# Attention scores computed two at a time, and attention's pieces placed inside the weight products

## The chip, the cores and the metric

The kernel runs on one NeuronCore of one Trainium2 chip. TensorE (PE in the profile; PEld is its weight load) multiplies, VectorE (DVE) and ScalarE (ACT) work element by element and read the products out of PSUM, GpSimd (POOL) does small sums, and the DMA queues bring the weights in. The metric is device time in microseconds (us), the median over runs of the whole program.

## The reference, cut to what matters

Two layers of a first block, then one second block, on a sequence of 256 tokens, 1024 wide, in fp32. A layer of the first block has a differential attention with 8 heads (two components of 64 each), a recurrent unit, a memory attention and an MLP. The second block has four attentions with 4 heads of 64 each.

```python
def diff_attention(q, k, v, lam, subln_g, lam_init):     # first block: 8 heads, two layers
    mask = key_chunk[None, :] <= q_chunk[:, None]         # chunks of 64 tokens, blocks of 128 queries
    s1 = jnp.einsum('bhqd,bhkd->bhqk', qb[0], k1).astype(jnp.float32) * scale
    s2 = jnp.einsum('bhqd,bhkd->bhqk', qb[1], k2).astype(jnp.float32) * scale
    p1 = jax.nn.softmax(jnp.where(mask, s1, NEG_BIG), axis=-1)
    p2 = jax.nn.softmax(jnp.where(mask, s2, NEG_BIG), axis=-1)
    p = p1 - lam * p2                                     # then p @ v

# second block: four branches of 4 heads each
o_sb = stick_breaking_attention(q, k, v)                  # strict causal, products of 1 - sigmoid
o_mb = moba_attention(q, k, v, t5_bias[:, :4])            # at this length one causal block with a bias
o_fx = forgetting_attention(q, k, v, f_logit)             # causal, plus sums of log f
o_ds = dsa_attention(q, k, v, q_idx, k_idx, w_idx, t5_bias[:, 4:])   # best 64 keys of an indexer, one k for all heads
```

## The kernel before

The weights are 267 blocks of up to 128 x 2048, in a fixed order (`plan`). For each block ScalarE rounds the block to fp32r (`wh`) and VectorE takes what is left over (`wl`); a product of a block is three passes on TensorE, `hi,wh`, `lo,wh` and `hi,wl`, which are 48 instructions of 128x256 for most blocks (24 of 128x512 for those that give token-major results). `step` emits one block: it reads out the last block's product (`flush`), lets light jobs run (`run_light`), lets up to `SEGS` = 3 attention pieces run (`run_heavy`), splits weights up to two blocks ahead (`pump`), and then emits the block's product (`mm`). The instructions of an engine are issued in the order in which they are emitted here.

An attention job is a Python generator: each `yield` ends a piece. For the differential attention (`attn_pair`, two heads) the pieces are scores of head 0; scores of head 1 and probabilities of head 0; transposes; the product with V; and so on. `run_heavy` walks through the waiting jobs in order of priority and runs one piece of each that has waited for `GAP` = 2 steps, unless the estimated lag of VectorE behind TensorE is over `ROOM`. So all pieces of a step stand in a row ahead of the step's product. `need` runs pieces of one branch without products between them until the branch is done.

Scores: queries and keys lie feature-major, so a head's (or a component's) 64 features are 64 of the 128 partitions. For each head or component there are two products, block t=0 (128 keys) and t=1 (256 keys), which use 64 rows of the PE array. The two components of a differential head, and the two heads of a pair in the second block, lie in the lower and the upper 64 partitions of the same tiles (`qk`; in the second block `f`). In block 1 the mask is a product with one row: `uvb[0:1]` holds a 1 for the first 64 queries and NEG for 64 keys, and it is added after each of the two products. In the second block masks are products of the identity `identb` with a bf16 mask (`diag`: `strictb`, `causalb`; or `add`, the choice of the indexer).

An fp32 product shows as two instructions in the trace, one of fp32r or bf16 as one. All calls go through one recording helper, so every instruction has that helper's line (L289 before) and groups are told apart by tiles. `ps` is a PSUM bank, from a pool of 8.

Of the kernel before, what the change touches and what calls it, by code (L numbers as in the profile page):

```python
# [19 lines left out]
NEG = -1e30  # L20
# [5 lines left out]
# ---------------------------------------------------------------- host side layout  # L26
# [43 lines left out]
def constants():  # L70
# [12 lines left out]
    u = np.zeros((128, 128), np.float32)  # L83
    u[0, :64] = 1.0
    v = np.zeros((128, 64), np.float32)
    v[0, :] = NEG
# [8 lines left out]
    c["cst"] = np.concatenate([ident, ident[::-1], rope, causal, strict, u, v], axis=1)  # L95
# [157 lines left out]
class Meter:  # L253
    """Passes an engine's calls on and books them on the clock."""
# [52 lines left out]
class Prog:  # L307
# [7 lines left out]
    def __init__(self, tc, A, out, pools):  # L315
# [10 lines left out]
        self.run_no = 0  # L326
        self.turned = []
        self.G = []

    # ---- tiles  # L330
# [12 lines left out]
    # ---- weight stream  # L343
# [37 lines left out]
    # ---- pacing  # L381
# [13 lines left out]
    def run_heavy(self, force=None):  # L395
        n = 0
        for h in list(self.heavy):
            if force is not None:
                if h[4] not in force:
                    continue  # L400
            elif n == self.SEGS or self.late() > self.ROOM:
                break
            elif self.clock - h[1] < h[3]:
                continue
            n += 1
            h[1] = self.clock
            if next(h[2], "end") == "end":
                self.heavy.remove(h)

# [5 lines left out]
    def step(self, mm, ev=None, early=None):  # L415
# [4 lines left out]
        self.run_heavy()  # L420
        self.clock += 1
        self.pump()
        mm()
# [35 lines left out]
    # ---- arithmetic helpers  # L459
# [17 lines left out]
    def mm_w2(self, banks, w, X, nk=8, p0=0, first=True, last=True, outer=False):  # L477
        """As mm_w, with a bank for each of the two blocks of columns; outer: one block after the other."""
# [81 lines left out]
    # ---- start  # L560
    def setup(self):
# [7 lines left out]
        cst = cp.tile([128, 960], F, name="cst")  # L569
# [34 lines left out]
        self.uvb = cp.tile([128, 192], BF, name="uvb")  # L604
# [6 lines left out]
    def setup_lam(self):  # L611
# [4 lines left out]
        nc.vector.tensor_copy(self.uvb, cst[:, 768:960])  # L616
# [46 lines left out]
    # ---- memory keys and values  # L663
# [36 lines left out]
    # ---- block 1  # L700
# [25 lines left out]
    def attn_pair(self, l, p, Q, K, V, Y):  # L726
# [208 lines left out]
    def wmany(self, key, js, X, ev, order, early=None):  # L935
        """Chunks js at once; order: (chunk, pair of rows) as they are multiplied."""
# [330 lines left out]
    # ---- block 2  # L1267
# [98 lines left out]
    def sb_head(self, h, Q, K, V, st):  # L1366
# [387 lines left out]
```

## Time and profile before

| | |
|---|---|
| runs, us | 1678.87 median of 3 (1678.62 to 1685.62) |
| the profiled execution | span 1679.4 us, 0.5 us above the median of the runs |
| PE busy | 1648.2 us (98%), 12400 instructions |
| DVE, ACT, POOL busy | 1057.0 (63%), 879.8 (52%), 98.0 (6%) |
| mean granted TensorE clock | 0.981 of full |
| DMA | 277.51 MB, 165 GB/s on the mean |

How to read it: PE is busy from end to end, so time is in what PE does and how densely it can do it; an average over the span says little of any one stage, and the stretches with attention have to be read by themselves. Matmuls overlap, so sums of their durations exceed the span; the distance from one start to the next is what a matmul costs.

### The profile page before, as it was taken

To read this page: it belongs to the slowest core of one execution; us is meant where nothing else is said; L and a number is where in the kernel's file an instruction comes from. 1 tells how busy PE (TensorE), PEld (TensorE's weight loads), DVE (VectorE), ACT (ScalarE), POOL (GpSimd) and SP (SyncE) were. 2 spreads that over 40 slices of the span, in tenths; PEclk is the share of its full clock that TensorE was granted. 3 is DMA by queue.
4 is the path that set the end of the run, shared out by engine and by line. 5 is a ranking of instruction groups with operands and counts; after the bars stand their busy time and mean duration, and the time that the engine had idled before them with its cause. 6 is when DMAs were issued, how large, how long until landed. Compare 5 with 4: busy or idle time off the path is not lost.

```text
span 1679.4 us, 28920 instructions
## 1 busy us (share of the span) xinstructions
PE 1648.2 (98%) x12400; PEld 1562.5 (93%) x12400; DVE 1057.0 (63%) x1400; ACT 879.8 (52%) x1207; POOL 98.0 (6%) x84
## 2 busy tenths in 40 slices
PE   8999999999999999999999999999999999999998
PEld 7887999999999998888999999999889998999997
DVE  6675676756755346756767656554377756578863
ACT  6344495545566345454864446653345544356542
POOL 1100000001100002000001102000120000000000
PEclk9998899999999999988999999999999999999999
DMA  8643244455445555432354543555434432436551
GB/s 299 217 161 124 76 151 151 160 193 207 170 177 188 188 203 215 160 126 76 126 170 166 202 176 144 183 201 176 164 127 174 164 138 101 175 133 220 179 179 70
DMA packets 42408, 277.51 MB, mean 165 GB/s; under 512 B 4800, under 2 KB 4936, under 8 KB 10536
## 3 DMA queue, kind: packets, MB, share of 16 engines
q1 hardware_dynamic: 41768, 274.21, 46.2%
q8 instruction: 97, 1.59, 0.4%
q0 software_dynamic: 512, 1.46, 0.3%
q14 instruction: 31, 0.25, 0.0%
HBM read 274.59 MB, written 1.06 MB: 164 GB/s over the span
## 4 chain that ended last, share of the span: by engine, by line
PE 90%; DVE 3%; issue 3%; ACT 2%; POOL 2%; DMA 0%; POOLq 0%; DVEq 0%; SPq 0%; ACTq 0%
PE ps L289 90%; POOL sq L289 1%; ACT wh L289 1%; DVE wl L289 1%; DVE x L289 0%; DVE lo L289 0%; ACT hi L289 0%; ACT sq L289 0%; DMA mem<-in_memT_dram 0%; DVE h L289 0%; ACT rl L289 0%; DVE at L289 0%; DVE g L289 0%; DVE isc L289 0%; DVE yg L289 0%
## 5 line engine op out<-in xcount | busy, mean ns | idle before, releaser
L289 PE MATMUL ps<-hi,wh 128*128 128x256 f32 x3312 | 949.6, 287 | 2.0 <-ACT hi L289 2.0
L289 PE MATMUL ps<-hi,wl 128*128 128x256 f32 x3312 | 941.0, 284 | 2.6 <-DVE wl L289 2.6
L289 PE MATMUL ps<-lo,wh 128*128 128x256 f32 x3312 | 938.4, 283 | 2.3 <-DVE lo L289 2.3
L289 DVE TENSOR_TENSOR wl<-ws,wh 128x2048 fp32r<-128x2048 f32 (+2 forms) x267 | 587.4, 2206 | 384.5 <-ACT wh L289 383.9
L289 PEld LDWEIGHTS ps<-hi,wh 128*128 128x128 f32 x3312 | 631.4, 191 | 6.1 <-ACT hi L289 2.6
L289 PEld LDWEIGHTS ps<-lo,wh 128*128 128x128 f32 x3312 | 632.0, 191 | 3.4 <-DVE lo L289 3.1
L289 PEld LDWEIGHTS ps<-hi,wl 128*128 128x128 f32 x3312 | 629.7, 190 | 3.4 <-DVE wl L289 3.4
L289 ACT ACTIVATE wh<-ws 128x2048 fp32r<-128x2048 f32 (+2 forms) x267 | 484.7, 1822 | 235.5 <-PE ps L289 212.1
L289 PE MATMUL ps<-wh,hi 128*128 128x512 f32 (+1 forms) x288 | 116.0, 403 | 8.9 <-ACT wh L289 7.0
L289 POOL TENSOR_TENSOR sq<-sq 128x512 f32<-128x512 f32 (+1 forms) x42 | 70.8, 1685 | 777.9 <-ACT sq L289 776.0
L289 PE MATMUL ps<-wh,lo 128*128 128x512 f32 (+1 forms) x288 | 114.4, 397 | 0.0
L289 PE MATMUL ps<-wl,hi 128*128 128x512 f32 (+1 forms) x288 | 114.3, 397 | 0.0
L289 PEld LDWEIGHTS ps<-wh,hi 128*128 128x128 f32 x288 | 55.8, 194 | 20.7 <-ACT wh L289 7.0
L289 PEld LDWEIGHTS ps<-wh,lo 128*128 128x128 f32 x288 | 55.5, 193 | 12.6 <-DVE lo L289 0.2
L289 PEld LDWEIGHTS ps<-wl,hi 128*128 128x128 f32 x288 | 55.8, 194 | 11.9 <-DVE wl L289 0.4
L289 DVE TENSOR_TENSOR lo<-rl,hi 128x512 fp32r<-128x512 f32 x32 | 23.3, 727 | 52.5 <-ACT hi L289 52.5
L289 DVE TENSOR_REDUCE at<-ps 128x1 f32<-128x128 f32 (+2 forms) x80 | 27.9, 386 | 44.6 <-PE ps L289 44.6
L289 ACT ACTIVATE rl<-ps 128x512 f32<-128x512 f32 (+1 forms) x40 | 22.6, 574 | 62.4 <-PE ps L289 62.4
L289 PE MATMUL ps<-ah,wh 128*128 128x256 f32 x176 | 49.7, 282 | 0.0
L289 PE MATMUL ps<-al,wh 128*128 128x256 f32 x176 | 49.6, 282 | 0.0
L289 PE MATMUL ps<-ah,wl 128*128 128x256 f32 x176 | 49.6, 282 | 0.0
L289 ACT ACTIVATE gz<-ps,hb 128x256 f32<-128x256 f32 x48 | 20.1, 469 | 49.5 <-PE ps L289 42.5
(230 smaller groups left out, 1337.1 us busy)
## 6 DMA issues: line engine op xcount, KB each, us to landing
ws<-in_up_dram SPq DMA_DIRECT2D x54, 1024.0 KB, 4.8
ws<-in_inw_dram SPq DMA_DIRECT2D x48, 1024.0 KB, 4.8
ws<-in_dn_dram SPq DMA_DIRECT2D x32, 1024.0 KB, 4.8
ws<-in_inq_dram SPq DMA_DIRECT2D x24, 1024.0 KB, 4.8
ws<-in_g_dram SPq DMA_DIRECT2D x16, 1024.0 KB, 4.9
ws<-in_wo_dram SPq DMA_DIRECT2D x12, 1024.0 KB, 4.8
ws<-in_in2f_dram SPq DMA_DIRECT2D x9, 1024.0 KB, 4.9
ws<-in_kvk_dram SPq DMA_DIRECT2D x8, 1024.0 KB, 5.4
```

The source lines that it names most:

```text
L289: return fn(*a, **k)
```

## The change

It does three things.

1. Scores in pairs. The products of two components (block 1) or two heads (second block) are emitted alternately into two banks: t=0 of the lower rows, t=0 of the upper rows, t=1 of the lower, t=1 of the upper. The second block's jobs are now for two heads each (`sb_heads`, `fox_heads`, `t5_heads`), with half as many jobs and pieces of twice the size.
2. Full-row masks. Block 1's mask is now `identb` times `lateb` (128 rows, 64 columns), and the four masks of a head follow after all its products, where each used to follow its product.
3. Pieces inside products. `run_heavy` runs one piece per call. It is called once ahead of the product, as before, and again inside it, when a third and two thirds of it have been passed.

```diff
     def run_heavy(self, force=None):
-        n = 0
+
         for h in list(self.heavy):
             if force is not None:
                 if h[4] not in force:
                     continue
-            elif n == self.SEGS or self.late() > self.ROOM:
+            elif self.late() > self.ROOM:
                 break
             elif self.clock - h[1] < h[3]:
                 continue
-            n += 1
             h[1] = self.clock
             if next(h[2], "end") == "end":
                 self.heavy.remove(h)
+            if force is None:
+                break
...
         self.run_heavy()
+        self.pump()
+        self.parts = [(n + 1) / self.SEGS for n in range(self.SEGS - 1)]
+        mm()
+        self.parts = []
         self.clock += 1
-        self.pump()
-        mm()
...
     def mid(self, part):
+        if self.parts and part >= self.parts[0] and part < 1.0:
+            self.parts.pop(0)
+            self.run_heavy()
...
         def scores(h):
             c0 = 4 * h
+            ss = [self.ps(), self.ps()]
+            for t in range(2):
+                o, n = 128 * t, 128 * (t + 1)
+                for c in range(2):
+                    rows = slice(c * 64, (c + 1) * 64)
+                    nc.tensor.matmul(ss[c][:, o:o + n], lhsT=q[rows, h, t * 128:(t + 1) * 128], rhs=k[rows, h, :n],
+                                     start=t == 0, stop=False, skip_group_check=True)
             for c in range(2):
-                s = self.ps()
-                rows = slice(c * 64, (c + 1) * 64)
                 for t in range(2):
-                    o, n = 128 * t, 128 * (t + 1)
-                    nc.tensor.matmul(s[:, o:o + n], lhsT=q[rows, h, t * 128:(t + 1) * 128], rhs=k[rows, h, :n],
-                                     start=t == 0, stop=False, skip_group_check=True)
-                    nc.tensor.matmul(s[:, o + n - 64:o + n], lhsT=self.uvb[0:1, 0:128], rhs=self.uvb[0:1, 128:192],
-                                     start=False, stop=True, skip_group_check=True)
+                    o = 256 * t + 64
+                    nc.tensor.matmul(ss[c][:, o:o + 64], lhsT=self.identb, rhs=self.lateb, start=False, stop=True,
+                                     skip_group_check=True)
+            for c in range(2):
+                s = ss[c]
...
-    def qk_scores(self, s, q, k, h, kk=None):
-        i, rows = divmod(h, 2)
-        rows = slice(rows * 64, rows * 64 + 64)
+    def qk_scores(self, q, k, i, kk=None):
+
+        ss = [self.ps(), self.ps()]
         for t, o, n in self.SEG:
-            self.nc.tensor.matmul(s[:, o:o + n], lhsT=q[rows, i, t * 128:(t + 1) * 128],
-                                  rhs=k[rows, i if kk is None else kk, :n],
-                                  start=t == 0, stop=False, skip_group_check=True)
+            for r in range(2):
+                rows = slice(r * 64, r * 64 + 64)
+                self.nc.tensor.matmul(ss[r][:, o:o + n], lhsT=q[rows, i, t * 128:(t + 1) * 128],
+                                      rhs=k[rows, i if kk is None else kk, :n],
+                                      start=t == 0, stop=False, skip_group_check=True)
+        return ss
...
+    def head_tail(self, i, ee, V, st, scale=1.0):
+        PT = [self.p_transpose(e, scale) for e in ee]
+        yield
+        for r in range(2):
+            self.attn_out(st, 2 * i + r, PT[r], V(2 * i + r))
...
-        for h in range(4):
-            self.spawn(self.t5_head(h, FT["dsq"], FT["kk"], lambda h: [VB[t][:, 256:320] for t in range(2)], 4, box,
+        for i in range(2):
+            self.spawn(self.t5_heads(i, FT["dsq"], FT["kk"], lambda h: [VB[t][:, 256:320] for t in range(2)], 4, box,
                                     BR[3]), 4, tag=3)
```

PE's rows in the first block, where the first scores of layer 0 stand. Before, behind the transposes of rotated keys (`rz`), two heads follow each other ahead of the next product; this is the first of them (`ps` numbers are banks by name, `LDWEIGHTS` loads a bf16 operand).

```order
L289 MATMUL ps_1236<-cst_86,rz_1093 128x128 x4
L289 MATMUL ps_1247<-qk_776,qk_727 128x128
L289 LDWEIGHTS uvb_109
L289 MATMUL ps_1247<-uvb_109 128x64
L289 MATMUL ps_1247<-qk_776,qk_727 128x256
L289 LDWEIGHTS uvb_109
L289 MATMUL ps_1247<-uvb_109 128x64
L289 MATMUL ps_1258<-qk_776,qk_727 128x128
L289 LDWEIGHTS uvb_109
L289 MATMUL ps_1258<-uvb_109 128x64
L289 MATMUL ps_1258<-qk_776,qk_727 128x256
```

The same head now stands inside the product into `ps_1167` (`hi` and `lo` are the activations, `wh` and `wl` the weights), with 18 more instructions of that product behind it, and then the other head.

```order
L287 MATMUL ps_1167<-hi_908,wl_1082 128x256
L287 MATMUL ps_1200<-qk_776,qk_727 128x128
L287 MATMUL ps_1201<-qk_776,qk_727 128x128
L287 MATMUL ps_1200<-qk_776,qk_727 128x256
L287 MATMUL ps_1201<-qk_776,qk_727 128x256
L287 LDWEIGHTS identb_106
L287 MATMUL ps_1200<-lateb_109,identb_106 128x64
L287 LDWEIGHTS identb_106
L287 MATMUL ps_1200<-lateb_109,identb_106 128x64
L287 LDWEIGHTS identb_106
L287 MATMUL ps_1201<-lateb_109,identb_106 128x64
L287 MATMUL ps_1167<-hi_908,wh_1081 128x256
```

What moved: the two components' products stand side by side in two banks, the masks behind them, and the product's instructions on both sides.

PE's rows in the second block, where `need` used to finish the forgetting attention (`fe` are its probabilities, `PT` their transposes, `V` the values) and the stick-breaking scores followed. Before, PE's transposes stand next to the products with V that read them, with no weight product between:

```order
L289 MATMUL ps_14104<-PT2_14012,V2_12365 64x128
L289 MATMUL ps_14108<-cst_86,fe_13804 128x128 x3
L289 MATMUL ps_14104<-PT2_14112,V2_12363 64x128 x2
L289 MATMUL ps_14104<-PT2_14112,V2_12365 64x128
L289 MATMUL ps_14123<-cst_86,fe_14021 128x128 x3
L289 MATMUL ps_14129<-cst_86,fe_14038 128x128 x3
L289 MATMUL ps_14104<-PT2_14127,V2_12363 64x128 x2
L289 MATMUL ps_14104<-PT2_14127,V2_12365 64x128
```

Now no such place is left. The stick-breaking pair, which followed there, stands inside a product, and the products with V stand in the run behind it:

```order
L287 MATMUL ps_13681<-hi_12562,wl_13526 128x256
L287 MATMUL ps_13750<-f2_13101,f2_13036 128x128
L287 MATMUL ps_13751<-f2_13101,f2_13036 128x128
L287 MATMUL ps_13750<-f2_13101,f2_13036 128x256
L287 MATMUL ps_13751<-f2_13101,f2_13036 128x256
L287 LDWEIGHTS identb_106
L287 MATMUL ps_13750<-strictb_108,identb_106 128x128
L287 LDWEIGHTS identb_106
L287 MATMUL ps_13751<-strictb_108,identb_106 128x128
L287 MATMUL ps_13681<-hi_12567,wh_13525 128x256
```

What moved: a second head's products stand beside the first's, and a transposed tile is read at least a run of products after it is made. Over the whole program PE now goes from weight products to attention pieces and back at 108 places (64 before), of which 64 read results of DVE or ACT.

## Rows read from the trace of the kernel before

**Rows 1.** The page: span, and busy time of each engine.
```profile
span 1679.4 us, 28920 instructions
PE 1648.2 (98%) x12400; PEld 1562.5 (93%) x12400; DVE 1057.0 (63%) x1400; ACT 879.8 (52%) x1207; POOL 98.0 (6%) x84
```

**Rows 2.** The page: shares of the chain that ended last.
```profile
PE 90%; DVE 3%; issue 3%; ACT 2%; POOL 2%; DMA 0%; POOLq 0%; DVEq 0%; SPq 0%; ACTq 0%
```

**Rows 3.** PE's waits: total us, times, longest.
```profile
PE ps L289 <- ACT PT L289: 1.1, 3, 0.6
```

**Rows 4.** Timeline of PE, one component's scores, block 1: start, us, operands, count.
```profile
178.26 0.49 PE L289 MATMUL ps<-qk 64*128 64x128 f32 x2
178.68 0.20 PE L289 MATMUL ps<-uvb 1*128 1x64 bf16 x1
178.80 0.70 PE L289 MATMUL ps<-qk 64*128 64x256 f32 x2
179.43 0.20 PE L289 MATMUL ps<-uvb 1*128 1x64 bf16 x1
179.56 0.37 PE L289 MATMUL ps<-qk 64*128 64x128 f32 x1
```

**Rows 5.** Windows, block 1's eight score stretches: length, busy by engine, PEclk, DMA.
```profile
132.76:139.34 6.58, 6.58 (x25) 3.64 (x25) 3.26 (x10) 3.67 (x16) 0.00 (x0) 0.75 0.74 308
...
178.26:183.47 5.21, 5.21 (x26) 3.08 (x25) 4.01 (x15) 2.85 (x12) 0.00 (x0) 1.00 0.02 8
...
sum 48.64, PE 48.64 PEld 27.46 DVE 27.53 ACT 25.39 POOL 0.00; mean PE 6.08 PEld 3.43 DVE 3.44 ACT 3.17 POOL 0.00
```

**Rows 6.** Windows, the eight runs of 48 products behind those stretches.
```profile
168.26:176.44 8.18, 8.18 (x50) 8.18 (x49) 4.78 (x11) 3.52 (x9) 0.00 (x0) 0.68 0.12 29
...
sum 60.16, PE 60.16 PEld 59.89 DVE 32.51 ACT 24.92 POOL 0.00; mean PE 7.52 PEld 7.49 DVE 4.06 ACT 3.12 POOL 0.00
```

**Rows 7.** Windows, a later run of 48 products, ahead of other pieces.
```profile
192.76:198.54 5.78, 5.78 (x52) 5.78 (x51) 4.76 (x16) 2.43 (x6) 0.00 (x0) 1.00 0.27 113
```

**Rows 8.** Timeline of PE, second block, two heads' scores emitted together.
```profile
1293.31 0.93 PE L289 MATMUL ps<-f,f 64*128 64x128 f32 x8
1294.17 0.39 PE L289 MATMUL ps<-hi,wh 128*128 128x256 f32 x1
```

**Rows 9.** Timeline of PE, second block, one head's scores, then its masks.
```profile
1323.33 0.92 PE L289 MATMUL ps<-f,f 64*128 64x128 f32 x4
1324.18 0.34 PE L289 MATMUL ps<-add,identb 128*128 128x128 bf16 x2
```

**Rows 10.** Timeline of PE, sums of the forgetting attention and its masks.
```profile
1387.30 0.92 PE L289 MATMUL ps<-cum,sel 4*128 4x128 f32 x4
1388.15 0.29 PE L289 MATMUL ps<-causalb,identb 128*128 128x128 bf16 x2
1388.36 0.37 PE L289 MATMUL ps<-f,f 64*128 64x128 f32 x1
```

**Rows 11.** Timeline of PE, two masks and the product behind them.
```profile
1410.92 0.28 PE L289 MATMUL ps<-strictb,identb 128*128 128x128 bf16 x2
1411.01 0.37 PE L289 MATMUL ps<-hi,wh 128*128 128x256 f32 x1
```

**Rows 12.** Windows, the second block's seven stretches of ds, fox and sb scores.
```profile
1386.45:1390.16 3.71, 3.71 (x22) 2.28 (x21) 0.79 (x3) 1.54 (x6) 0.00 (x0) 1.00 0.63 254
1401.06:1404.14 3.08, 3.08 (x20) 1.87 (x19) 1.43 (x3) 2.44 (x5) 0.00 (x0) 1.00 0.00 0
...
sum 15.54, PE 15.54 PEld 9.60 DVE 8.72 ACT 6.49 POOL 0.00; mean PE 2.22 PEld 1.37 DVE 1.25 ACT 0.93 POOL 0.00
```

**Rows 13.** Timeline of PE, transposes and the product with V behind them.
```profile
1396.82 0.55 PE L289 MATMUL ps<-cst,fe 128*128 128x128 f32 x3
1397.95 0.32 PE L289 MATMUL ps<-PT,V 128*64 128x128 f32 x1 [0.58 <-ACT PT L289]
```

**Rows 14.** Windows, layer 0's stretch of scores and the products between.
```profile
132.00:192.00 60.00, 60.00 (x318) 47.99 (x317) 31.23 (x81) 28.13 (x86) 0.00 (x0) 0.80 0.26 91
```

More of the change, by code (lines that the diff above doesn't have):

```diff
@@ L82, in constants @@
     strict = np.where(k < q, 0.0, NEG).astype(np.float32)
[L83 to L86, printed above, removed]
+    late = np.zeros((128, 64), np.float32)
+    late[:64] = NEG
     dist = 255 - np.arange(384)
@@ L94, in constants @@
         sel[h, h * 128:(h + 1) * 128] = -8.0
-    c["cst"] = np.concatenate([ident, ident[::-1], rope, causal, strict, u, v], axis=1)
+    c["cst"] = np.concatenate([ident, ident[::-1], rope, causal, strict, late], axis=1)
     c["cst2"] = np.concatenate([hot, dead, sel], axis=1)
@@ L420, in step @@
         self.run_heavy()
+        self.pump()
+        self.parts = [(n + 1) / self.SEGS for n in range(self.SEGS - 1)]
+        mm()
+        self.parts = []
         self.clock += 1
-        self.pump()
-        mm()
         if ev is not None:
@@ L568, in setup @@
         self.P = cp.tile([128, NPAR], F, name="P")
-        cst = cp.tile([128, 960], F, name="cst")
+        cst = cp.tile([128, 832], F, name="cst")
         lamv = self.t(name="lamv").rearrange("p a b -> p (a b)")
@@ L603, in setup @@
         self.strictb = cp.tile([128, 128], BF, name="strictb")
-        self.uvb = cp.tile([128, 192], BF, name="uvb")
+        self.lateb = cp.tile([128, 64], BF, name="lateb")
         self.zeros = cp.tile([128, 256], F, name="zeros")
@@ L615, in setup_lam @@
         nc.vector.tensor_copy(self.strictb, cst[:, 640:768])
-        nc.vector.tensor_copy(self.uvb, cst[:, 768:960])
+        nc.vector.tensor_copy(self.lateb, cst[:, 768:832])
         self.neglam = cp.tile([128, 2], F, name="neglam")
@@ new lines, in sb_heads @@
+    def sb_heads(self, i, Q, K, V, st):
+        nc = self.nc
+        ss = self.qk_scores(Q, K, i)
+        for s in ss:
+            self.diag(s, self.strictb)
+        ee = []
+        for s in ss:
+            th, pr, E = (self.t(name="sb", shape=(128, 512)) for _ in range(3))
+            nc.scalar.activation(th[:, :384], s[:, :384], AF.Tanh, scale=0.0625)
+            nc.scalar.activation(pr[:, :384], th[:, :384], AF.Identity, scale=-0.5, bias=self.half)
+            nc.gpsimd.memset(E[:, 127:128], 1.0)
+            nc.gpsimd.memset(E[:, 383:384], 1.0)
+            for a, b in ((0, 127), (128, 383)):
+                nc.vector.tensor_tensor_scan(E[:, a:b][:, ::-1], pr[:, a + 1:b + 1][:, ::-1],
+                                             self.zeros[:, :b - a], 1.0, op0=OP.mult, op1=OP.add)
+            nc.vector.scalar_tensor_tensor(E[:, :384], th[:, :384], 1.0, E[:, :384], op0=OP.add, op1=OP.mult)
+            ee.append(E)
@@ L1380, in sb_head, with fox_heads @@
         yield
-        PT = self.p_transpose(E, 0.5)
-        yield
-        self.attn_out(st, h, PT, [V[t][:, h * 64:h * 64 + 64] for t in range(2)])
-    def fox_head(self, h, Q, K, V, box, st):
+        yield from self.head_tail(i, ee, V, st, 0.5)
+    def fox_heads(self, i, Q, K, V, box, st):
         nc = self.nc
@@ L1389, in fox_head, with t5_heads @@
         c = box["c"]
-        s = self.ps()
-        self.qk_scores(s, Q, K, h)
-        for t, o, n in self.SEG:
-            nc.tensor.matmul(s[:, o:o + n], lhsT=self.sel[0:4, h * 128:(h + 1) * 128], rhs=c[0:4, :n],
-                             start=False, stop=False, skip_group_check=True)
-        self.diag(s, self.causalb)
-        e = self.t(name="fe", shape=(128, 512))
-        ls, r = self.softmax_from(s, e, 0.125)
+        ss = self.qk_scores(Q, K, i)
+        for r, s in enumerate(ss):
+            h = 2 * i + r
+            for t, o, n in self.SEG:
+                nc.tensor.matmul(s[:, o:o + n], lhsT=self.sel[0:4, h * 128:(h + 1) * 128], rhs=c[0:4, :n],
+                                 start=False, stop=False, skip_group_check=True)
+        for s in ss:
+            self.diag(s, self.causalb)
+        ee = [self.t(name="fe", shape=(128, 512)) for _ in ss]
+        lr = [self.softmax_from(s, e, 0.125) for s, e in zip(ss, ee)]
         yield
-        self.softmax_scale(e, ls, r)
+        for e, (ls, r) in zip(ee, lr):
+            self.softmax_scale(e, ls, r)
         yield
-        PT = self.p_transpose(e)
-        yield
-        self.attn_out(st, h, PT, [V[t][:, h * 64:h * 64 + 64] for t in range(2)])
-    def t5_head(self, h, Q, K, V, g0, box, st):
+        yield from self.head_tail(i, ee, V, st)
+    def t5_heads(self, i, Q, K, V, g0, box, st):
         nc = self.nc
@@ L1550, in gate_ev @@
             return ev
-        for h in range(4):
-            self.spawn(self.t5_head(h, FT["dsq"], FT["kk"], lambda h: [VB[t][:, 256:320] for t in range(2)], 4, box,
+        for i in range(2):
+            self.spawn(self.t5_heads(i, FT["dsq"], FT["kk"], lambda h: [VB[t][:, 256:320] for t in range(2)], 4, box,
                                     BR[3]), 4, tag=3)
```

64 lines of the change are left out of this document (27 added, 37 removed).

## The prediction

> **What bounds the kernel now.** I read the page first: PE is busy for 1648.2 of 1679.4 us [rows 1] and makes up 90% of the chain that ended last [rows 2]. PE's list of waits, the second view, holds almost nothing inside the attention: the one entry there is the wait for a transposed tile, 1.1 us in three times [rows 3]. So nothing PE waits for can be worth much, and a gain must come from what PE itself does. Third, the timeline of PE and the windows, stage by stage. In most of the program a run of 48 products takes 5.78 us at full clock [rows 7], 0.12 us each. Two things stand out against that.
>
> The first is what a score costs. One component of block 1 takes from 178.26 to 179.56, 1.30 us: two products on 64 rows and two masks on one row [rows 4]. A head of the second block has the same two products with no mask between them, and takes 0.85 us (1323.33 to 1324.18) [rows 9]. The columns are the same but for the masks, so the alternation between 64 rows and one row costs most of the 0.45.
>
> The second is the clock. There are eight stretches of scores in block 1, two heads each, four per layer; together 48.64 us. The one from 178.26 runs at a granted clock of 1.00 and takes 5.21; the one from 132.76 runs at 0.75 on the mean and takes 6.58 [rows 5]. The low level is 1.2 GHz, the other 2.4. The run of products behind each is caught as well: 60.16 us for eight, one of them 8.18 at 0.68 [rows 6], against 5.78 at 1.00 [rows 7]. In the second block, stretches of 3.71 and 3.08 us of scores with full-row masks stay at 1.00 [rows 12]. So what the clock follows here is the dense alternation of block 1, not scores as such.
>
> **The change part by part.**
>
> *Scores of block 1.* Sixteen heads, two components each. What two score products side by side cost is in the trace, since the `mb` jobs of the second block already emit two heads in one step: 8 instructions, two heads, take 0.86 us from 1293.31 to the next product at 1294.17 [rows 8], as long as one head alone. The upper 64 rows are free. The four new masks (128 rows, 64 columns) have no row. The nearest are two masks of 128 columns: 0.09 with products behind them [rows 11], 0.21 with 64-row work behind them [rows 10]. Here products follow, so I take 0.2 for four, between 0.09 (narrow ones cost half) and 0.42. A head then costs 0.86 + 0.2 = 1.06, sixteen 17.0 us (15.2 to 20.5). Were the components not to overlap, a head would be 2 x 0.85 + 0.2 = 1.9 and all 30.4. Against 48.64 now: **-31.6 us**. Of this, 8 x 5.21 = 41.7, so 24.7 is structure and 7.0 is clock.
>
> A rule of the Trainium skill speaks against the full overlap: TensorE: Matmul & The Clock Gate, "Part 3: Packing small matmuls — row/col tiling" ("The mechanism"), says that matmuls start and end strictly in program order, with only weight loads pulled ahead. By it the second component's first pass could start only behind the first's second pass, an estimated quarter of 0.85 us per pair would stay single, and 22 pairs (16 and the second block's 6) would gain 4.7 us less, 1633, which is inside the forecast's own range. The trace does not agree: before, the two `mb` heads stand one wholly behind the other in program order, and yet take the time of one. The sum goes by the row.
>
> *Products at the low clock.* If the score stretches no longer pull the clock down, the eight runs fall from 60.16 to 8 x 5.78 = 46.24: **-13.9 us**. Why they should not: a head's scores are now 1.06 us with both halves of the array at work, and the next head stands behind at least 6 products (mostly 18, 2.1 us), where today 5.2 us of scores follow each other. The second block's 3 to 4 us stretches at 1.00 [rows 12] are longer than anything that is left in block 1. This is the step I trust least, since no row has such a mixture.
>
> *Second block.* The seven stretches of ds, fox and sb scores take 15.54 us [rows 12]. In pairs: two ds pairs of 0.86 + 0.3 (wider masks), two fox pairs of 0.86 + 2 x 0.85 for the sums of both heads, which stay on the same four rows [rows 10], + 0.2, two sb pairs of 1.06: 2.3 + 5.5 + 2.1 = 9.9. **-5.6 us** (without overlap 0). The `mb` pairs are paired already: 0.
>
> *Pieces inside products.* The places where a product with V reads tiles transposed just ahead go away, and with them PE's wait, **-1.1 us** [rows 3]; one such wait is 1.13 us from transposes to V [rows 13]. Every piece does the same work on DVE and ACT as before. Going into 64-row work costs PE about 0.12 us (two masks, 0.21 with such work behind them against 0.09 [rows 10, 11]); there are eight more such places in block 1 (16 heads apart, in place of eight stretches): **+1.0 us**. For other pieces the run of 48 products in front shows no price (5.78, 0.12 each) [rows 7]; 44 more places at an upper 0.12 would be 5.3, which I keep for the range.
>
> *Nothing:* the constant load is narrower and the cast of `uvb` becomes a smaller one of `lateb`; both lie under the first products, long before the first score. If their cover were gone it would be under half a us.
>
> Sum: -31.6 - 13.9 - 5.6 - 1.1 + 1.0 = -51.2. The profiled span is 0.5 above the runs' median, so against the median 1678.9 - 51 = **1628 us**.
>
> **What is queued behind.** DVE and ACT are in-order. A mid-run piece's maximum waits on DVE until PE has come to that part of the run, and the next read-out of a product queues behind it. In layer 0's stretch DVE has 31.23 us of work and ACT 28.13 in 60.00 [rows 14]; if the stretch shrinks by half of the first two terms (22.8) to 37.2, DVE is at 84% there. That is close, but weights are split two blocks ahead, so a lag of a few us is hidden; if it is not, PE waits for a bank.
>
> **The rivals.**
>
> *The clock falls anyway* (0.12). For: bursts on 64 rows, fp32 transposes and masks are still there, now closer together with few products between. Against: the second block's stretches at 1.00 [rows 12]. Full persistence gives back 7.0 + 13.9 = 20.9: 1649; half of it 1638.
>
> *No overlap in block 1's order* (0.05). The trace has the pair as t0, t1, t0, t1; the new order alternates. Then block 1 gains 48.64 - 30.4 = 18.2, of the second block's 5.6 nothing, and with the clock's 13.9 and the rest the time is about 1647.
>
> *PE waits for banks or read-outs* (0.09). Two banks per piece and up to three pieces in a step, of 8 banks. Each of the 22 paired bursts waiting 0.6 us, as long as PE's longest wait for a transposed tile [rows 3], gives 13: 1641; twice that 1655.
>
> *Slower* (0.03). A piece inside a run holds up the products behind it when its input is late. There are 64 places that read DVE or ACT. Were each to expose the full 1.13 us from transposes to V [rows 13], that is +72 against -51, about 1700. It decides from 0.8 us per place. Against: between a piece and the next of its job there are still at least 1.3 runs of products, over 7 us.
>
> *Better* (0.03): masks at the low bound and no price for entries: 1625, or less where the second head's sums overlap too.
>
> **How the numbers follow.** The forecast has the rest, 0.68, and by itself 1622 to 1636 (masks from 15.2 to 20.5, entries up to 5.3). For 8 in 10 and the unknown clock and banks the range reaches to 1645 above, which leaves out the full persistence of the low clock and the larger bank waits, and to 1619 below, the better case less the 7 us by which the three runs before differ. A measurement of this kernel tells about 0.5% (8 us) from no change. All cases but the slower one, and a little of the bank waits grown large, are faster by more: 0.95; within it 0.02; slower 0.03.
>
> **What would show it.** In the profile after: two components' eight `qk` instructions within about 0.9 us, the masks 0.2 behind them; granted clock 1.00 from 132 to 190 and in the same stretch of layer 1, and the runs of products there at 0.12 each; no PE wait for PT; PE's total busy time down by some 50 and DVE's and ACT's unchanged. I am wrong if the clock row shows low stretches between scores, if pairs take 1.7 us, or if PE's waits list grows by an entry for banks or for DVE in the attention.

## The result, and the profile after

The changed kernel takes 1635.92 us (median of 4 runs, 1630.47 to 1636.40), the kernel before 1681.57 in runs beside it (1678.62 to 1685.62): ratio 0.9717, interval 0.9693 to 0.9742, faster. The profiled spans are 1679.4 and 1634.4, a gain of 45.0 us where 51.2 were forecast. The page of the changed kernel (span, busy time):

```profile
span 1634.4 us, 28931 instructions
PE 1600.3 (98%) x12400; PEld 1532.0 (94%) x12400; DVE 1053.4 (64%) x1400; ACT 876.1 (54%) x1207; POOL 94.4 (6%) x84
```

Against [rows 1] PE has 47.9 us less work with the same number of instructions; DVE's and ACT's stays. The scores of the first head, both components of what [rows 4] shows for one component of a later head, stand in the timeline of PE with the product around them:

```profile
128.99 0.28 PE L287 MATMUL ps<-hi,wl 128*128 128x256 f32 x1
129.20 0.93 PE L287 MATMUL ps<-qk 64*128 64x128 f32 x8
130.06 0.29 PE L287 MATMUL ps<-lateb,identb 128*128 128x64 bf16 x4
130.18 0.37 PE L287 MATMUL ps<-hi,wh 128*128 128x256 f32 x1
130.39 0.28 PE L287 MATMUL ps<-lo,wh 128*128 128x256 f32 x1
```

Read the starts: two components take 129.20 to 130.06, 0.86 us, the four masks 0.12. The product's last instruction ahead of the piece takes 0.21 to the next start (128.99 to 129.20) and the first one behind it 0.21 as well (130.18 to 130.39), where others take 0.12 [rows 7]. So this place costs 0.18 us beside its own work.

To see where the 45.0 us lie, I cut each trace at the same weight products into three stretches that hold the attention: layer 0, layer 1, second block. Windows of the kernel before (length, busy time of PE, PEld, DVE, ACT, POOL, then granted clock, DMA share, GB/s):

```profile
89.48:383.89 294.41, 294.41 (x2099) 273.70 (x2098) 197.29 (x302) 163.86 (x268) 6.14 (x4) 0.96 0.41 146
683.98:990.19 306.21, 306.21 (x2182) 284.24 (x2180) 202.30 (x294) 168.54 (x271) 11.38 (x12) 0.96 0.44 151
1242.63:1443.53 200.90, 199.59 (x1582) 184.40 (x1580) 136.19 (x251) 95.85 (x142) 0.53 (x8) 1.00 0.42 147
sum 801.52, PE 800.21 PEld 742.35 DVE 535.77 ACT 428.25 POOL 18.05; mean PE 266.74 PEld 247.45 DVE 178.59 ACT 142.75 POOL 6.02
```

and of the changed kernel:

```profile
90.39:363.55 273.16, 272.42 (x2100) 259.03 (x2099) 195.47 (x302) 162.13 (x268) 4.71 (x4) 1.00 0.44 158
663.61:949.73 286.12, 284.35 (x2182) 269.20 (x2181) 200.71 (x294) 167.22 (x271) 9.24 (x12) 1.00 0.45 161
1204.88:1397.69 192.81, 192.81 (x1581) 181.44 (x1580) 135.54 (x250) 94.91 (x142) 0.53 (x8) 1.00 0.43 152
sum 752.09, PE 749.58 PEld 709.67 DVE 531.73 ACT 424.26 POOL 14.48; mean PE 249.86 PEld 236.56 DVE 177.24 ACT 141.42 POOL 4.83
```

The attention gave 49.4 us: 21.3 and 20.1 in the layers, 8.1 in the second block. The clock is at 1.00 in all three, where it was at 0.96 in the layers. The rest of the program, which the change hardly touches, went from 877.9 to 882.3: 4.4 us were lost there. PE's list of waits has two new entries that belong to the attention (total, times, longest), and that for `PT` [rows 3] is gone:

```profile
PE ps L287 <- ACT me L287: 1.4, 1, 1.4
PE ps L287 <- ACT ti L287: 0.4, 1, 0.4
```

In each layer a wait of 0.3 us for `lo` comes on top, which the kernel before does not have there.

### The profile page after: what moved, and what is told of

The parts are those of the page before. It is cut to its first block, busy times and chain, and to the rows that moved or that the text cites. A ratio compares the mean times of both kernels' runs of the same rounds, so it can differ in the third digit from the quotient of the medians.

```text
span 1634.4 us, 28931 instructions
## 1 busy us (share of the span) xinstructions
PE 1600.3 (98%) x12400; PEld 1532.0 (94%) x12400; DVE 1053.4 (64%) x1400; ACT 876.1 (54%) x1207; POOL 94.4 (6%) x84
## 3 DMA queue, kind: packets, MB, share of 16 engines
HBM read 274.52 MB, written 1.06 MB: 169 GB/s over the span
## 4 chain that ended last, share of the span: by engine, by line
PE 83%; DVE 6%; ACT 4%; issue 3%; POOL 2%; DMA 1%; SPq 0%; POOLq 0%; DVEq 0%; ACTq 0%
PE ps L287 83%; DVE wl L287 2%; ACT wh L287 2%; POOL sq L287 1%; DVE xc L287 1%; DVE s L287 1%; ACT hi L287 1%; DVE lo L287 1%; DMA ws<-in_kvv_dram 1%; DVE x L287 0%; SPq L287 0%; ACT sq L287 0%; ACT me L287 0%; DVE gz L287 0%; ACT gz L287 0%
## 5 line engine op out<-in xcount | busy, mean ns | idle before, releaser
L287 ACT ACTIVATE e<-ps,at 128x128 f32<-128x128 f32 x64 | 26.0, 421 | 44.9 <-DVE at L287 44.9
```

Of the source, the lines that this page charges most:

```text
L287: return fn(*a, **k)
```

## The experiments

Ratios are to the kernel before on the same chip; "attention" is the sum of the three stretches above. A place is where PE goes from weight products to other work and back; a fall is a stretch at half the clock (0.50). In the code, `...` marks what is left out.

**Pairs and masks without the spreading.** `run_heavy` and `step` as before, so up to three pieces stand in a row ahead of the product. This is called the row kernel below.

```diff
...
         self.run_heavy()
+        self.clock += 1
         self.pump()
-        self.parts = [(n + 1) / self.SEGS for n in range(self.SEGS - 1)]
         mm()
-        self.parts = []
-        self.clock += 1
...
```

> The changed kernel with paired scores and full-row masks, but pieces in a row ahead of the product as before (85 places where PE goes from products to pieces and back, in place of 138). Theory A, as predicted: the clock fell because of the dense change between 64 rows and one row, so the masks and pairs alone return it, and spreading the pieces only costs entries: 1630 to 1636, granted clock 1.00 in both score stretches, no more PE waits than 1.1 us for PT. Rival B: it is the spreading that returns the clock: two paired heads, transposes and masks in a row still pull it down, stretches at 0.7 to 0.8, and of the 13.9 us in the products behind at least half come back: 1643 to 1652.

Measured: 1625.89 us (1625.52 to 1626.83), ratio 0.9661 (0.9646 to 0.9677), wholly below the changed kernel's interval. Its windows:

```profile
89.56:361.11 271.55, 271.55 (x2100) 258.59 (x2098) 195.82 (x302) 162.34 (x268) 6.14 (x4) 1.00 0.45 159
661.23:944.55 283.32, 283.32 (x2181) 269.07 (x2180) 200.74 (x294) 167.08 (x271) 11.40 (x12) 1.00 0.47 163
1198.79:1387.94 189.15, 189.15 (x1581) 179.62 (x1579) 135.40 (x250) 94.60 (x142) 0.53 (x8) 1.00 0.44 156
sum 744.02, PE 744.02 PEld 707.28 DVE 531.96 ACT 424.02 POOL 18.08; mean PE 248.01 PEld 235.76 DVE 177.32 ACT 141.34 POOL 6.03
```

The clock is back without any spreading, and the attention is 8.1 us shorter than in the changed kernel. Theory A holds for the clock, and the time is below its 1630 to 1636: the spreading costs more than I had allowed for.

**Spreading alone.** The kernel before with the new `run_heavy`, `step` and `mid`, nothing else of the change.

> The kernel before with only the pieces spread inside the products: components one after the other, one-row masks between their products, single heads in the second block. Theory A (the kind of work pulls the clock down): a head's scores are still 2.6 us of changes between 64 rows and one row, 16 times, so the clock still falls for part of them, while the structure's 24.7 us stay lost: 1668 to 1685. Rival B (the density of pieces pulls it down): with products between all heads the clock is 1.00, 20.9 us come back less 3 to 5 us for the new entries: 1661 to 1664.

Measured: 1675.90 us (1673.93 to 1680.08), ratio 0.9957 (0.9944 to 0.9971): theory A.

```profile
89.43:376.56 287.13, 286.79 (x2100) 267.79 (x2098) 196.52 (x302) 164.03 (x268) 4.71 (x4) 0.99 0.42 150
676.62:978.83 302.21, 301.80 (x2181) 280.32 (x2180) 201.82 (x294) 169.05 (x271) 9.26 (x12) 0.98 0.44 153
1231.35:1436.94 205.59, 204.39 (x1582) 186.74 (x1580) 136.28 (x250) 96.10 (x142) 0.53 (x8) 1.00 0.42 146
```

With products between the heads the clock rises from 0.96 to 0.99 and 0.98, not to 1.00, and the layers gain 11.3 us. The second block, at 1.00 before and after, loses 4.7: there the spreading shows its price without the clock. It is not a price of entries alone. From start to start the scores take 1.7 us more there and the products with V 1.4, since some of both that stood side by side now stand apart: the `mb` heads, two in 0.86 us [rows 8], take 0.85 each (1277.97 to 1278.82 for one).

**Order within a pair.** The two loops exchanged, in block 1 (shown) and in the second block, so that a component's or head's two products are emitted before the other's.

```diff
-            for t in range(2):
-                o, n = 128 * t, 128 * (t + 1)
-                for c in range(2):
+            for c in range(2):
+                for t in range(2):
...
```

> The changed kernel with the two components' (and heads') products emitted one wholly behind the other (t0, t1 of the lower rows, then t0, t1 of the upper), masks still behind all. If a product may start while an earlier one in program order has not started, as the rows of the kernel before showed it: 0.86 us per pair, no change, 1633 to 1639 (within 0.2%). Rival (starts strictly in program order): of 22 pairs each loses about a quarter of 0.85 us, 4.7 us, 1640 to 1642, and the upper rows' first product starts at least 0.3 us behind the lower rows' first.

Measured: 1637.27 us (1635.10 to 1640.46), ratio 0.9729 (0.9709 to 0.9750). Timeline of the first head:

```profile
128.99 0.93 PE L287 MATMUL ps<-qk 64*128 64x128 f32 x8
129.86 0.29 PE L287 MATMUL ps<-lateb,identb 128*128 128x64 bf16 x4
```

0.87 us, as in alternate order, and the time is in the range of the first expectation. Layer 0 takes 273.20 and the second block 192.91, as in the changed kernel. Layer 1 takes 2.8 us more: PE waits 2.38 for `me` there in place of 1.4, and from the end of that wait the clock is at half for 3.4 us. The row of the wait, and the window behind it:

```profile
769.68 1.12 PE L287 MATMUL ps<-cst,me 128*128 128x128 f32 x4 [2.38 <-ACT me L287]
```

```profile
769.69:773.10 3.41, 3.41 (x16) 3.41 (x17) 2.15 (x6) 3.34 (x8) 0.00 (x0) 0.50 0.59 247
```

In the first head of layer 0 the starts come in pairs 13 ns apart, the four of 128 columns ahead of the four of 256, although the program has 128, 256, 128, 256. The Trainium skill (TensorE: Matmul & The Clock Gate, "Part 3: Packing small matmuls — row/col tiling", "The mechanism") has matmuls start and end in strict program order; for the starts this trace does not agree.

**One-row masks again, behind all products of the head**, pieces spread as in the changed kernel.

```diff
-   nc.tensor.matmul(ss[c][:, o:o + 64], lhsT=self.identb, rhs=self.lateb, start=False, stop=True,
+   nc.tensor.matmul(ss[c][:, o:o + 64], lhsT=self.uvb[0:1, 0:128], rhs=self.uvb[0:1, 128:192], start=False, stop=True,
```

> The changed kernel with block 1's masks as one-row products again (ones times a row of NEG), but behind all products of the head, in place of identity times a full-row mask. Theory A (changes between 64 rows and one row cost, not the one-row product): a head has one such change in place of four per component, 0.1 to 0.4 us more than now, so 16 heads cost 2 to 6 us: 1637 to 1642, clock 1.00. Rival (one-row products are what pulls the clock down or drains PE): low stretches come back in the attention, 1645 to 1656.

Measured: 1633.99 us (1632.34 to 1634.48), ratio 0.9707 (0.9687 to 0.9726); attention 752.37 against 752.09, clock 1.00. The clock stays up with one-row masks behind the products, so the rival is out. Theory A's price shows in the timeline: a head's four masks take 0.21 us to the next start, where four full-row ones take 0.12.

```profile
128.81 0.28 PE L289 MATMUL ps<-uvb 1*128 1x64 bf16 x4
129.02 0.39 PE L289 MATMUL ps<-hi,wh 128*128 128x256 f32 x1
```

That is 1.4 us for sixteen heads, a little under theory A's 2 to 6. It does not show in the time because PE's idle time in the layers is 1.3 us less here than in the changed kernel (1.22 against 2.51, length less busy time of the windows).

**One edit to the kernel before.** Its one-row masks moved behind the head's products; no alternation, no spreading, single heads in the second block.

```diff
-   for c: for t: product(c, t); mask(c, t)      # the loops, written short
+   for c: for t: product(c, t)
+   for c: for t: mask(c, t)
```

> The kernel before with one edit: block 1's four one-row masks of a head stand behind the head's four products instead of one behind each product. Pieces in a row ahead of the product, single heads in the second block, as before. Theory A (the change from 64 rows to one row and back keeps the components apart and lowers the clock): the two components now overlap and the clock stays at 1.00, so all of block 1's gain comes with this edit alone: against the row kernel of the first experiment it lacks the 5 to 6 us of the second block, 1630 to 1635. Rival (the full-row mask or the spreading is needed for the clock): 1645 to 1656, low stretches in the attention.

Measured: 1638.82 us (1637.32 to 1639.84), ratio 0.9745 (0.9725 to 0.9765).

```profile
90.05:361.95 271.90, 271.90 (x2099) 258.71 (x2098) 195.87 (x302) 162.25 (x268) 6.14 (x4) 1.00 0.45 158
662.02:945.76 283.74, 283.74 (x2182) 269.30 (x2181) 200.85 (x294) 167.04 (x271) 11.38 (x12) 1.00 0.47 163
1199.30:1401.70 202.40, 201.09 (x1582) 185.82 (x1581) 135.88 (x250) 95.83 (x142) 0.53 (x8) 0.99 0.41 145
```

In both layers this is the row kernel to 0.4 us: moving the masks is all of block 1's gain. The time was 4 us over theory A since pairs are worth 13.2 us in the second block (202.40 against 189.15; one fall of 3.4 us included), where I had said 5 to 6.

**Full-row masks between the components**, in the row kernel: each component's masks right behind its own products.

> The row kernel of the first experiment with each component's two full-row masks right behind its own two products, so that full-row work stands between the components. Theory A (full-row work between two half-height bursts ends their overlap, and the clock falls from changes with one-row work, not from half-height work): a head costs 2 x (0.85 + 0.2) in place of 1.0, 16 heads 16 to 18 us more, clock 1.00: 1641 to 1645. Rival B (half-height work in long stretches, 4.2 us for two heads, lowers the clock whatever stands between): the clock falls as in the kernel before, up to 20 us more, 1652 to 1665. Rival C (a full-row mask does not part them): 1626 to 1629.

Measured: 1645.46 us (1643.99 to 1645.84), ratio 0.9784 (0.9768 to 0.9801).

```profile
89.44:370.09 280.65, 280.65 (x2099) 264.30 (x2098) 197.12 (x302) 163.64 (x268) 6.15 (x4) 0.99 0.44 153
670.16:964.08 293.92, 293.92 (x2182) 276.28 (x2181) 202.32 (x294) 168.29 (x271) 11.38 (x12) 0.99 0.45 157
```

Timeline of the first head:

```profile
132.72 0.92 PE L287 MATMUL ps<-qk 64*128 64x128 f32 x4
133.57 0.23 PE L287 MATMUL ps<-lateb,identb 128*128 128x64 bf16 x2
133.73 0.92 PE L287 MATMUL ps<-qk 64*128 64x128 f32 x4
```

Full-row work between them parts the components: one takes 1.01 us, where both together took 0.98. The layers take 19.7 us more, a little over theory A's 16 to 18. Part of it is the clock, at 0.99, which that theory had at 1.00: it falls three times in these two stretches, 3.4 us each, with no one-row work anywhere. So the overlap follows theory A, the clock does not.

**The same with one-row masks.**

> The kernel in which each component's masks stand behind its own two products, with one-row masks in place of full-row ones. Theory A (the clock follows how long the array stays half empty, whatever parts the components): as with full-row masks there, 1641 to 1650, with three to five falls of the clock in the attention. Rival B (one-row work in between lowers the clock by itself): falls at all eight stretches of scores as in the kernel before, 1652 to 1665.

Measured: 1653.13 us (1648.38 to 1657.86), ratio 0.9822 (0.9798 to 0.9847).

```profile
89.38:374.92 285.54, 285.54 (x2100) 268.94 (x2099) 197.23 (x302) 163.70 (x268) 6.14 (x4) 0.98 0.43 151
674.98:972.37 297.39, 297.39 (x2182) 279.48 (x2180) 202.15 (x294) 168.28 (x271) 11.38 (x12) 0.98 0.45 155
```

Six falls in the layers and one in the second block, between the three above and the eight of the kernel before: neither theory's number, though the time is in the rival's range. In the layers the clock is at half for 27.3 us, against 10.2 above and 47.8 in the kernel before, and the 8.4 us by which they are longer than above are about half of the difference. Full-row masks between components came with falls; one-row masks there came with more. The mean clock of the four runs says the same, 0.985 to 0.989 here and 0.990 to 0.993 above.

**Three pieces at one place inside the product**, at its middle, and none ahead (`parts = [0.5]`).

> The changed kernel with up to three pieces in a row at one place of a product, its middle, and none ahead of it (88 places where PE goes to pieces and back; the row kernel has 85, the changed kernel 138). Theory A (each place costs about 0.12 us whether it stands inside a product or ahead of it): like the row kernel, 1625 to 1629. Rival (standing inside a product costs, since results come later or read-outs are held up): like the changed kernel, 1633 to 1637, with PE waits for DVE or ACT in the attention.

Measured: 1635.20 us (1632.10 to 1636.84), ratio 0.9723 (0.9704 to 0.9742): the rival. Attention 752.47 with 88 places, where the row kernel has 85 and takes 744.02. PE's waits from 80 to 1000 us, which holds both layers, the largest entry; then one of them in the timeline, and a window close behind it:

```profile
PE ps L287 <- ACT hi L287: 4.1, 2, 2.5
```

```profile
311.41 0.38 PE L287 MATMUL ps<-hi,wh 128*128 128x256 f32 x1 [2.46 <-ACT hi L287]
```

```profile
313.11:316.52 3.41, 3.41 (x19) 3.41 (x18) 2.90 (x2) 1.97 (x2) 0.00 (x0) 0.50 0.11 17
```

The row kernel has no such wait there. The waits, 4.1, and the low clock (3.4 us at half, 1.7 lost) are 5.8 of the 7.4 us by which the two layers are longer. So a count of places does not tell the time by itself; where they stand decides what PE then waits for.

**Sums of the forgetting attention in pairs.** In the row kernel, a copy of the sums and of `sel` on rows 64 to 67 for the second head.

```diff
...
-   lhsT=self.sel[0:4, h * 128:(h + 1) * 128], rhs=c[0:4, :n]
+   lhsT=self.sel[b:b + 4, h * 128:(h + 1) * 128], rhs=c[b:b + 4, :n]      # b = 64 * r, heads alternate
```

> The row kernel of the first experiment with the forgetting attention's sums of the two heads of a pair on rows 0 to 3 and on rows 64 to 67 and emitted alternately, in place of both on rows 0 to 3. Theory A (work on disjoint rows overlaps whatever its height): a pair's eight instructions take 0.86 us in place of 1.7, 1.7 us in all, 1623 to 1626, seen in the timeline of the sums. Rival (only 64-row work overlaps): unchanged, 1.7 us per pair.

Measured: 1626.19 us (1624.70 to 1628.87), ratio 0.9673 (0.9655 to 0.9691): too small to see in the time; the attention is 0.9 us shorter (743.16). Timeline of the row kernel, then of this one:

```profile
1262.37 1.57 PE L287 MATMUL ps<-cum,sel 4*128 4x128 f32 x8
1263.88 0.40 PE L287 MATMUL ps<-causalb,identb 128*128 128x128 bf16 x4
```

```profile
1261.73 0.92 PE L287 MATMUL ps<-cum,sel 4*128 4x128 f32 x8
1262.59 0.40 PE L287 MATMUL ps<-causalb,identb 128*128 128x128 bf16 x4
```

1.51 to 0.86 us per pair, theory A: work of four rows overlaps as well, and four rows cost what 64 do.

**Products with V alternately**, on top of that.

```diff
-        for r in range(2):
-            self.attn_out(st, 2 * i + r, PT[r], V(2 * i + r))
+        for a, b, t in blocks:           # the three products of a head, written short
+            for r in range(2):           # outputs in partitions 0..63 and 64..127
+                matmul(st["o"][r * 64:r * 64 + 64, ...], lhsT=V(2 * i + r)[t], rhs=PT[r][:, a:b])
```

> The row kernel with the paired sums, and in the second block the products with V of a pair's two heads emitted alternately (their outputs lie in the lower and the upper 64 partitions of one bank). Theory A (products whose outputs take different 64 columns of the array overlap as those on different 64 rows do, and alternate order lets all twelve of a pair overlap, where head after head only part of them do): a pair goes from 1.07 us to about 0.85, eight pairs 1.5 to 2 us, 1622 to 1626. Rival (the overlap in pairs is complete, the rest is entry and exit): no change in the sum of PT,V, 7.3 us.

Measured: 1623.58 us (1622.23 to 1626.42), ratio 0.9649 (0.9634 to 0.9664), the fastest here, beside 1634.81 of the changed kernel run again. A single head in the kernel before, then a pair head after head, and alternately:

```profile
1396.02 0.87 PE L289 MATMUL ps<-PT,V 128*64 128x128 f32 x6
1396.82 0.55 PE L289 MATMUL ps<-cst,fe 128*128 128x128 f32 x3
```

```profile
1315.78 1.15 PE L287 MATMUL ps<-PT,V 128*64 128x128 f32 x12
1316.86 0.39 PE L287 MATMUL ps<-hi,wh 128*128 128x256 f32 x1
```

```profile
1317.43 0.88 PE L287 MATMUL ps<-PT,V 128*64 128x128 f32 x12
1318.24 0.39 PE L287 MATMUL ps<-hi,wh 128*128 128x256 f32 x1
```

One head takes 0.80 us, a pair 1.08 and 0.81. Products on different output columns overlap too, and here the order does matter. The second block went from 188.30 to 187.02.

**Up to five pieces in a row**, on top of that (`SEGS = 5`).

> The kernel with paired sums and alternate products with V, with up to five pieces in a row ahead of a product in place of three (72 places where PE goes to pieces and back, in place of 85). Theory A (each place costs 0.06 to 0.24 us, nothing else changes): 1 to 3 us less, 1620 to 1624. Rival (longer rows make PE wait for tiles from ACT and DVE, or pull the clock down): 1626 to 1640, with waits for PT or new low stretches in the attention.

Measured: 1649.03 us (1648.58 to 1651.74), ratio 0.9801 (0.9787 to 0.9816): the rival, and worse than its range. Attention 768.77 in place of 742.10, with 72 places. PE's waits from 80 to 1000 us, the longest of them, and a window around its end:

```profile
PE ps L287 <- ACT ti L287: 12.2, 6, 4.2
```

```profile
193.17 0.58 PE L287 MATMUL ps<-hi,wh 128*128 128x256 f32 x1 [4.18 <-ACT ti L287]
```

```profile
191.85:198.67 6.82, 5.50 (x25) 5.50 (x26) 4.81 (x12) 5.84 (x10) 0.00 (x0) 0.50 0.42 155
```

The wait is not for a tile that a piece or the product reads. By its releaser the next product waits until ACT has read `ti` out of a bank, and ACT comes to that late, behind the `PT` copies and a weight split. The clock falls around such waits: three stretches of 6.8 us at half clock in the attention.

**The changed kernel again.**

> The changed kernel again, beside the others on one chip: 1630 to 1637. If the falls of the clock between layer 1 and the second block come by chance, their number or length differs from the two of 6.8 us in the first profile.

Measured: 1634.81 us (1632.86 to 1636.36), ratio 0.9710 (0.9693 to 0.9727). Attention 752.11 against 752.09. Low stretches between layer 1 and the second block, first profile, then this one:

```profile
1174.79:1181.61 6.82, 5.65 (x19) 5.26 (x20) 6.65 (x15) 2.83 (x6) 0.00 (x0) 0.50 0.00 0
1195.27:1202.09 6.82, 6.49 (x30) 6.49 (x31) 1.83 (x2) 2.76 (x3) 1.14 (x3) 0.50 0.48 183
```

```profile
1174.98:1178.39 3.41, 3.41 (x12) 3.12 (x13) 3.34 (x7) 1.42 (x3) 0.00 (x0) 0.50 0.00 0
1195.46:1198.87 3.41, 3.41 (x19) 3.41 (x18) 0.00 (x0) 2.70 (x3) 0.83 (x2) 0.50 0.65 269
```

The same kernel at the same places, with half the low time. The first profile has one more fall ahead of these (3.4 us from 980.23), which the second has not, and the second one behind the attention (6.8 us from 1434.39), which the first has not. These falls differ from one execution to the next.

## Why the prediction was right, and where it was off

The forecast was 1628, within 1619 to 1645; 1635.9 came. By its steps:

- **Scores of block 1** (-31.6): a head takes 0.98 us with its masks, forecast 1.06. Sixteen are 15.7, so -32.9. The row with the two `mb` heads [rows 8] was the right witness. The alternation that the change writes adds nothing (exchanged loops), the masks' place does it all (masks moved alone).
- **Products at the low clock** (-13.9): right in amount: the clock is 1.00 through both layers, and this and the term above, forecast at 45.5 together, gave 45.8 in the row kernel's layers, where no spreading is in the way. The reason was half right. Dense alternation with one-row work is not the whole cause: full-row masks between components bring falls too, and one-row masks behind all products bring none. In the layers there are eight falls in the kernel before, six and three in those with masks between components, four in the one with the spreading alone: in all of these the components run one after the other, each on half of the array's rows. Where they overlap, the layers have none, except that one (exchanged loops), one (the middle) and two (five in a row) came at PE waits of 2.4 to 4.2 us. That the half-empty array is what lowers the clock fits these counts, but it is argued, not shown. Why one-row work between makes it worse is open, and a wait of that size alone was not tried. I took the second block's stretches at 1.00 [rows 12] for a firmer witness than they are. The kernel with only the masks moved has the same second block as the kernel before, and there the clock falls at 1346.60, behind 3.5 us of the scores and sums that ran at 1.00 for 3.71 us in [rows 12]. The kernel with one-row masks between components has a fall at 1294.32 behind 5.4 us of paired scores and sums, which the kernel with full-row masks there ran at 1.00. PE waits at neither. So such a stretch brings a fall in one execution and none in another, and the argument from [rows 12] was weaker than it looked, though what it was used for came true.
- **Entries into 64-row work** (+1.0): this is the term that was mis-sized. I priced an entry at 0.12 for eight places and read "no price" for other pieces off the run in [rows 7]. That run has `Km,qm` behind it, full-row work, which indeed costs nothing. At a score PE pays on both sides, 0.18 us in the timeline above. Against the row kernel the changed one has 53 more places (138 against 85 by the experiments' count; the 108 and 64 ahead of the prediction are a smaller count) and takes 8.1 us more in the attention, 7.1 more than this term. In the layers it is 4.4: 2.5 is PE's idle time, which the row kernel does not have there (273.16 less 272.42 and 286.12 less 284.35 in the windows; `me` and `ti` are most of it). The forecast had such waits at nothing and priced them only among the rivals. The other 1.9 are not split up by any run: fourteen more changes from products straight into a score, at 0.18, would be 2.5 at most, since the row kernel pays on entry too where a head follows other full-row work (0.20 from the last transpose to the score in place of 0.11). The second block's 3.7 come without a wait: fifteen more places, and pairs of products with V apart where two pairs could stand together, which is 1.2 of it (8.57 against 7.35 us from start to start). What the spreading saved, the wait for `PT`, the row kernel saves as well, by having two heads per job; the kernel with only the masks moved, with one, still has it.
- **Second block** (-5.6 and -1.1): -8.1 came, -11.8 in a row. I missed that the two heads' products with V, next to each other in one job, overlap on their columns: all of them together take 9.96 us from start to start in the kernel before, 8.57 in the changed one and 7.35 in a row.
- **The rest of the program** was taken as unchanged; it came out 4.4 longer. 2.7 are between layer 1 and the second block, where the first profile has three falls, 17.1 us together, and the kernel before has two, 10.2; but the second profile, with the 6.8 us shown above, is still 1.4 longer there than the kernel before, so the clock is not all of it. Over all fourteen profiles the part outside the attention lies between 877.9 and 882.5, with the kernel before at the low end. So some 4 us of the shortfall lie outside the stretches that the edit is about. Whether it has a part in them is not shown: the changed kernel came out at 882.3 and 882.5, the kernel before was profiled once, and the other kernels with pieces inside products lie between 878.7 and 881.8.

Together: 51.2 forecast; two layers 3.1 short (44.5 against 41.4), second block 1.4 better, the rest 4.4 lost: 45.1. The inner range, 1622 to 1636, was made of masks and entries, and its lower end does not follow from them (masks at the low bound and no entries give 1625); the outer one's lower end is 1625 less 7, which is 1618 and not 1619. That the time came just inside its upper end owes more to the rest of the program, 4.4, than to either.

Of the three signs of being wrong that the prediction named, the third came, in small: PE's list of waits did grow in the attention, by four waits, 2.5 us in all. The other two did not.

**The rivals.** The clock's fall did not persist. "No overlap" is excluded by the changed kernel's own timeline, 0.86 us for two components in alternate order, and the exchanged loops show that the order does not matter. PE's new waits cost about 2.5 us, not 13; with five pieces in a row that rival is what happens, 12.2 us of waits for a bank. "Slower", pieces that wait at many places for late input, shows in no run: `me`, 1.4 us, is its only case in the changed kernel. "Better", no price for entries, 1625, is the time that the kernel without spreading reaches, in part by products with V that this case did not have.

## What to carry to other kernels

Here products on different halves of the array's rows ran at the price of one (0.86 us for two heads' scores, 0.85 for one), and those on different halves of its output columns did so in alternate order (0.81 us for two heads' products with V, 0.80 for one). A mask between them, of one row or of 128, ended that; look for a mask or a transpose in between, move it behind both, and measure starts in the timeline. With the components paired, the clock stayed at 1.00 in both layers without any spreading, and spreading small pieces through a large product then cost 8.1 us in entries, waits and pairs taken apart: try the pairing without the spreading. Compare stretches cut at the same instructions rather than spans when a few us matter, since low-clock stretches elsewhere come and go between executions.

## What was not expected of the hardware

Four-row products cost as much as 64-row ones and overlap on disjoint rows (1.51 to 0.86 us per pair). Two heads' products with V overlap on output columns, fully only in alternate order (1.08 against 0.81 us, one head alone 0.80), while score products on separate rows overlap in either order (0.86 and 0.87). The attention's stretches repeat to 0.02 us between two executions of one kernel (752.09 and 752.11), so differences of 1 us there can be read from a single trace as long as no fall is in it: the same second block took 189.24 us without a fall and 190.77 with one, in the two kernels with masks between components.
